# Two of the four weight-quadrant sums of a Winograd feed-forward matmul made by accumulating DMAs instead of VectorE

## Chip, cores, metric

The kernel runs on one core of a Trainium2 chip, as one program. The metric is the device time of one execution in microseconds (us); lower is better. The engines are TensorE (PE: matmuls; PEld: its weight loads), VectorE (DVE), ScalarE (ACT), GpSimd (POOL) and SyncE (SP, which only issues DMAs here).

## What is computed

One layer of a streaming encoder on 512 tokens of width 1024: an adaLN-modulated norm, an input projection that feeds a gMLP branch and an mLSTM branch, an output projection and a gated residual; then the part that matters here, a modulated norm and a squared-ReLU MLP of inner width 4096:

```python
xn = modulate(rmsnorm(h, norm2_g[l]), sh2, sc2)
ff = jnp.square(jax.nn.relu(xn @ w_ff1[l])) @ w_ff2[l]
h = h + g2[:, None, :] * ff
return rmsnorm(h, final_g)
```

`xn` is 512 x 1024, `w_ff1` 1024 x 4096, `w_ff2` 4096 x 1024, all in 32-bit floats.

## The kernel before

Every large matmul runs in three passes. Each operand is split into a high part, rounded to PE's fp32r format by a cast on ScalarE, and a low part, the difference, from VectorE; `mm3` (lines 106 to 109) then issues high x high, high x low and low x high into one PSUM bank. A weight piece of 512 KB is thus loaded by SP into a staging buffer (pool `raws`, tag "raw", three buffers), cast (line 908 in the changed part: wh), subtracted (line 909: wl) and used. The pairs wh and wl have three buffers each.

The first feed-forward matmul, `xn @ w_ff1`, is done in eight groups n of 512 of the 4096 columns. Group 0 is multiplied directly (`block0`, banks f10b, weight splits f100 to f106, activations x2h/x2l), first for the first half of the tokens and then for the second. Groups 1 to 7, called blocks below, use Winograd's form of Strassen's algorithm: the weights of a block are cut in quadrants B11, B12, B21, B22 (rows kh by columns nh, each held as 128 partitions x 4 x 256), the activations in A11 (first tokens, first half of the width), A12, A21 (second tokens), A22, and seven products replace eight:

- activation sums, made once ahead of the loop: S1 = A21 + A22, S2 = S1 - A11, S3 = A11 - A21, S4 = A12 - S2 (line 974, split in lines 976 and 977);
- weight sums, made per block by VectorE: T1 = B12 - B11 (line 928), T2 = B22 - T1 (line 930), T3 = B22 - B12 (line 934), T4 = B21 - T2 (line 937);
- products in this order, each 24 matmuls of 128x256 in one PSUM bank (`product`): P1 = A11 B11, P6 = S2 T2, P2 = A12 B21, P7 = S3 T3, P5 = S1 T1, P4 = A22 T4, P3 = S4 B22;
- the results are put together from the banks by one copy on ScalarE (line 1005) and six additions on VectorE (lines 1006 to 1016), and `relu2` applies relu and square on ScalarE.

`operands()` is a generator that yields the split operands in the order of the products; `product` draws them so that the split of an operand is ordered three products ahead of its use, and its cast waits until the product three places ahead of it has released its wh buffer. The loads of a block's quadrants are issued two at a time at two places of the block before (`load_quads`, line 902). B11 and B21 go to the staging buffers (tag "raw", 3), B12 and B22 to pool `x2p` (tag "q", 3). T1 and T2 take the two buffers of tag "sc" in pool `fp`, which held the scaled token tiles `sc2` of the norm (`resid_norm`, lines 814 to 825: the residual is added in lines 819 and 820, squared and summed in 822, GpSimd makes the reciprocal root in lines 72 and 73, and VectorE scales in line 824). T3 is written over B12.

A scheduler orders the instructions of each engine when the program is built. On the chip every engine runs its list in order, and so do the two that issue DMAs: an instruction that waits holds up all that stands behind it on that engine. Names with numbers, such as T21, are a tile and its block: T2 of block 1.

Of the kernel before, what the change touches and what calls it, by code (L numbers as in the profile page):

```python
# [16 lines left out]
P = 128  # L17
# [29 lines left out]
def block_kernel(ctx, tc, vecs_d, rows_d, ws_d, x_d, w_ada, w_in, w_out, w_ff1, w_ff2, out_d):  # L47
    nc = tc.nc
    act, dve, pool, pe, sp = nc.scalar, nc.vector, nc.gpsimd, nc.tensor, nc.sync

    const = ctx.enter_context(tc.tile_pool(name="const", bufs=1))
    raws = ctx.enter_context(tc.tile_pool(name="raws", bufs=3))
# [665 lines left out]
    for half in range(2):  # L718
# [4 lines left out]
        if half == 0:  # L723
            for t in range(TB):
                dve.scalar_tensor_tensor(out=vg[t], in0=vg[t], scalar=gmv[:, t, 0:1], in1=lng,
                                         op0=ALU.subtract, op1=ALU.mult)
                dve.scalar_tensor_tensor(out=vg[t], in0=vg[t], scalar=grs[:, t:t + 1], in1=lnb,
                                         op0=ALU.mult, op1=ALU.add)
        for t in range(TB):
            act.activation(ug[t][:, cs], b[t], AF.Gelu_apprx_tanh)  # L730
        for g in range(4 * half, 4 * half + 4):
# [33 lines left out]
    fp = ff.enter_context(tc.tile_pool(name="ffp", bufs=1))  # L765
# [36 lines left out]
    for k in range(KT):  # L802
# [35 lines left out]
    x2p = x2s.enter_context(tc.tile_pool(name="x2p", bufs=1, side="right"))  # L838
# [9 lines left out]
    def ring(nm, dt=F32, shape=(2, 256)):  # L848
        return fp.tile([P] + list(shape), dt, tag="hT", name=nm, bufs=32)
# [19 lines left out]
    def half_op(pr, kh):  # L869
        return lambda kt: tuple(v[:, kt % 2] for v in x2[pr, 2 * kh + kt // 2])  # L870
# [7 lines left out]
    for k0 in range(0, KT, 2):  # L878
        raw = raws.tile([P, 2, 512], F32, tag="raw", name=f"raw_f10{k0}")
# [15 lines left out]

    hq = {}

    def quad(n, kh, nh):
        pl_, tg, bf = (x2p, "q", 3) if nh else (raws, "raw", 3)
        raw = pl_.tile([P, 4, 256], F32, tag=tg, name=f"B{n}{kh}{nh}", bufs=bf)  # L900
        c0 = n * 512 + nh * 256
        sp.dma_start(out=raw, in_=w_ff1[kh * 512:(kh + 1) * 512, c0:c0 + 256].rearrange("(k p) c -> p k c", p=P))
        return raw

    def op_split(src, nm):
        wh = wpool.tile([P, 4, 256], F32R, tag="wh", name="wh_" + nm)
        wl = wpool.tile([P, 4, 256], F32R, tag="wl", name="wl_" + nm)
        act.copy(out=wh, in_=src)  # L908
        dve.tensor_sub(out=wl, in0=src, in1=wh.bitcast(F32))  # L909
        return wh, wl  # L910

    NB = FF // 512
    quads = {}

    def load_quads(n, kh):
        if n < NB:
            for nh in range(2):
                quads[n, kh, nh] = quad(n, kh, nh)

    def operands():  # L920
        for n in range(1, NB):
            if n == 1:
                load_quads(n, 0)
                load_quads(n, 1)
            b11, b12, b21, b22 = (quads[n, kh, nh] for kh in range(2) for nh in range(2))
            yield op_split(b11, f"B11{n}")
            t1 = fp.tile([P, 4, 256], F32, tag="sc", name=f"T1{n}", bufs=2)
            dve.tensor_sub(out=t1, in0=b12, in1=b11)
            t2 = fp.tile([P, 4, 256], F32, tag="sc", name=f"T2{n}", bufs=2)
            dve.tensor_sub(out=t2, in0=b22, in1=t1)  # L930
            load_quads(n + 1, 0)
            yield op_split(t2, f"T2{n}")
            yield op_split(b21, f"B21{n}")
            dve.tensor_sub(out=b12, in0=b22, in1=b12)
            yield op_split(b12, f"T3{n}")
            yield op_split(t1, f"T1{n}")
            dve.tensor_sub(out=t2, in0=b21, in1=t2)
            yield op_split(t2, f"T4{n}")
            load_quads(n + 1, 1)
            yield op_split(b22, f"B22{n}")  # L940

    ops_ = operands()
    opq = []

# [14 lines left out]
    for k in range(KT):  # L959
        block0(1, k)  # L960

    def relu2(dst, src):
        act.activation(dst, src, AF.Relu)
        act.activation(dst, dst, AF.Square)

    for pr in range(2):
# [2 lines left out]
    sx = {}  # L969
    for kp in range(2):  # L970
        a11, a12, a21, a22 = xn[0, kp], xn[0, kp + 2], xn[1, kp], xn[1, kp + 2]
        for nm, op, dst, i0, i1 in (("S1", dve.tensor_add, a22, a21, a22), ("S3", dve.tensor_sub, a21, a11, a21),
                                    ("S2", dve.tensor_sub, a11, a22, a11), ("S4", dve.tensor_sub, a12, a12, a11)):
            op(out=dst, in0=i0, in1=i1)
            hl = mp.tile([P, 2, 2, 256], F32R, tag="mv", name=f"{nm}hl{kp}", bufs=8)
            act.copy(out=hl[:, 0], in_=dst)
            dve.tensor_sub(out=hl[:, 1], in0=dst, in1=hl[:, 0].bitcast(F32))
            sx[nm, kp] = hl
    prefetch_op(2)
    for pr in range(2):  # L980
        for nh in range(2):
            relu2(hq[0, nh, pr], fb[pr][nh].rearrange("p (f t) -> p f t", f=2))

    def sum_op(nm):
        return lambda kt: tuple(sx[nm, kt // 2][:, q, kt % 2] for q in range(2))

    def product(xop, nm):
        prefetch_op(3)
        wh, wl = opq.pop(0)
        bk = bank(nm)  # L990
        for kt in range(4):
            xh_, xl_ = xop(kt)
            for f in range(2):
                fs = slice(f * P, (f + 1) * P)
                mm3(bk[:, f * 256:(f + 1) * 256], wh[:, kt, fs], wl[:, kt, fs], xh_, xl_, kt == 0 and f == 0,
                    kt == 3 and f == 1)
        prefetch_op(2)
        return bk.rearrange("p (f t) -> p f t", f=2)

    for n in range(1, NB):  # L1000
        c = {(nh, th): ring(f"h{n}{nh}{th}") for nh in range(2) for th in range(2)}
        for key, v in c.items():
            hq[(n,) + key] = v
        c11, c12, c21, c22 = c[0, 0], c[1, 0], c[0, 1], c[1, 1]
        act.copy(out=c11, in_=product(half_op(0, 0), f"P1{n}"))
        dve.tensor_add(out=c12, in0=c11, in1=product(sum_op("S2"), f"P6{n}"))
        dve.tensor_add(out=c11, in0=c11, in1=product(half_op(0, 1), f"P2{n}"))
        relu2(c11, c11)
        dve.tensor_add(out=c21, in0=c12, in1=product(sum_op("S3"), f"P7{n}"))
        p5 = product(sum_op("S1"), f"P5{n}")  # L1010
        dve.tensor_add(out=c22, in0=c21, in1=p5)
        dve.tensor_add(out=c12, in0=c12, in1=p5)
        relu2(c22, c22)
        dve.tensor_add(out=c21, in0=c21, in1=product(half_op(1, 1), f"P4{n}"))
        relu2(c21, c21)
        dve.tensor_add(out=c12, in0=c12, in1=product(sum_op("S4"), f"P3{n}"))
        relu2(c12, c12)

    ws_ff = Stream([(w_ff2[k * P:(k + 1) * P, :], 1, D, f"f2{k}") for k in range(FF // P - LAST)], 2)
    ws_ff.prefetch(2)  # L1020
# [52 lines left out]
    for t in range(TB):  # L1073
        sc = fp.tile([P, D], F32, tag="sc", name=f"sc3{t}", bufs=2)
        zs = []
        for hf in range(2):
# [70 lines left out]
```

## Time and profile before

| what | value |
|---|---|
| median of 2 runs | 835.91 us (835.77 to 836.05) |
| span of the profiled execution, first to last instruction | 834.4 us |
| PE busy, share of the span | 822.7 us, 99% |
| VectorE busy | 553.4 us, 66% |
| ScalarE busy | 359.5 us, 43% |
| GpSimd busy | 42.2 us, 5% |
| mean granted TensorE clock | 0.995 |
| 512 KB quadrant loads of the changed loop | 28, median 3.8 us to landing |

The runs list no separate time of the profiled execution; its span stands 1.5 us below the median of the runs. Times in the text are us from the start of that span. In the profile, a group's row gives busy time and mean ns, then the engine's idle time ahead of the group and what ended it; a timeline row gives the start, the duration, the engine, the line, the operation and what it writes and reads; tile names there carry no numbers. The loop over blocks 1 to 7 runs from 506.7 to about 648 us, some 20.2 us a block.

### The profile page before, as it was taken

What the parts mean: (1) busy time and instruction counts of PE and PEld (TensorE: products, weight loads), DVE (VectorE), ACT (ScalarE), POOL (GpSimd) and SP (SyncE); (2) the same over time, 40 slices, a digit from 0 to 9 for tenths busy, and PEclk for the clock granted to TensorE, in tenths of its full rate; (3) what the DMA queues carried; (4) which work ended last, traced back from release to release, by engine and by line L of the source; (5) the groups of instructions that cost most, each with busy time, mean ns of one, the idle gap of its engine ahead of it and who ended that gap; (6) DMA issues with size and microseconds to landing.
All of it is one profiled execution on the core that took longest, in us unless ns stands there. A gap on an engine that the chain in (4) does not pass through costs nothing.

```text
span 834.4 us, 11373 instructions
## 1 busy us (share of the span) xinstructions
PE 822.7 (99%) x4427; PEld 700.2 (84%) x4427; DVE 553.4 (66%) x857; ACT 359.5 (43%) x540; POOL 42.2 (5%) x60
## 2 busy tenths in 40 slices
PE   8999999999999999999999999999999999999996
PEld 6887888887888888888888899999999888888885
DVE  5979657584733377888566689888888434443546
ACT  5557456274333233222444456666666221221314
POOL 2003020130100000100000000000000000000000
PEclk9999999999999999999999999999999999999998
DMA  9973331143033398676344231333321422222302
GB/s 274 269 239 107 105 97 26 43 135 101 3 98 101 114 340 290 211 266 218 106 179 144 84 122 49 105 108 114 106 77 65 138 101 101 78 99 101 111 15 102
DMA packets 66822, 107.28 MB, mean 129 GB/s; under 512 B 5328, under 2 KB 38224, under 8 KB 66768
## 3 DMA queue, kind: packets, MB, share of 16 engines
q1 hardware_dynamic: 66768, 106.56, 39.6%
q8 instruction: 35, 0.57, 0.3%
q14 instruction: 19, 0.16, 0.1%
HBM read 104.44 MB, written 2.10 MB: 128 GB/s over the span
## 4 chain that ended last, share of the span: by engine, by line
PE 94%; ACT 1%; DMA 1%; issue 1%; DVE 1%; POOL 0%; SPq 0%; POOLq 0%; DVEq 0%
PE ob L108 7%; PE ob L109 7%; PE ob L107 7%; PE P L107 6%; PE P L108 6%; PE P L109 6%; PE qk L273 4%; PE wo L107 1%; PE wo L108 1%; PE wo L109 1%; PE cp L232 1%; PE k1b L107 1%; PE u1b L107 1%; PE mv1b L109 1%; PE gb0b L108 1%
## 5 line engine op out<-in xcount | busy, mean ns | idle before, releaser
L107 PE MATMUL ob<-wh_f,hsh 128*128 128x512 f32 x240 | 94.9, 395 | 0.0
L108 PE MATMUL ob<-wl_f,hsh 128*128 128x512 f32 x240 | 94.9, 395 | 0.0
L109 PE MATMUL ob<-wh_f,hsl 128*128 128x512 f32 x240 | 94.9, 395 | 0.0
L85 ACT CAST wh_f<-raw_f 128x1024 fp32r<-128x1024 f32 x28 | 29.5, 1053 | 115.2 <-PE ob L109 112.1
L86 DVE TENSOR_TENSOR wl_f<-raw_f,wh_f 128x1024 fp32r<-128x1024 f32 x28 | 34.3, 1225 | 58.2 <-ACT wh_f L85 57.1
L107 PEld LDWEIGHTS ob<-wh_f,hsh 128*128 128x128 f32 x240 | 45.2, 188 | 10.8
L108 PEld LDWEIGHTS ob<-wl_f,hsh 128*128 128x128 f32 x240 | 45.2, 188 | 10.8
L109 PEld LDWEIGHTS ob<-wh_f,hsl 128*128 128x128 f32 x240 | 45.2, 188 | 10.8
L908 ACT CAST wh_T<-T 128x1024 fp32r<-128x1024 f32 x21 | 22.0, 1049 | 24.3 <-PE P L108 23.4
L107 PE MATMUL P<-x2h,wh_B 128*128 128x256 f32 x112 | 31.7, 283 | 0.0
L108 PE MATMUL P<-x2l,wh_B 128*128 128x256 f32 x112 | 31.6, 282 | 0.0
L109 PE MATMUL P<-x2h,wl_B 128*128 128x256 f32 x112 | 31.4, 280 | 0.0
L908 ACT CAST wh_B<-B 128x1024 fp32r<-128x1024 f32 x21 | 22.1, 1051 | 18.1 <-PE P L108 16.7
L1027 DVE CAST hsh<-h 128x512 fp32r<-128x512 f32 x30 | 12.7, 426 | 25.6 <-PE ob L108 25.6
L909 DVE TENSOR_TENSOR wl_T<-T,wh_T 128x1024 fp32r<-128x1024 f32 x21 | 25.7, 1225 | 2.9 <-ACT wh_T L908 2.9
L909 DVE TENSOR_TENSOR wl_B<-B,wh_B 128x1024 fp32r<-128x1024 f32 x21 | 25.6, 1221 | 0.5 <-ACT wh_B L908 0.5
L86 DVE TENSOR_TENSOR wl_gb<-raw_gb,wh_gb 128x1024 fp32r<-128x1024 f32 x8 | 9.8, 1224 | 20.7 <-ACT wh_gb L85 20.7
L1028 DVE TENSOR_TENSOR hsl<-h,hsh 128x512 fp32r<-128x512 f32 x30 | 20.7, 691 | 3.0 <-DVE hsh L1027 0.5
L651 DVE SCALAR_TENSOR_TENSOR accg<-arg,c_act,accg 128x1024 f32<-128x1024 f32 x14 | 17.9, 1282 | 5.2 <-DMA arg<-in_w_ada 5.0
L109 PEld LDWEIGHTS P<-x2h,wl_B 128*128 128x128 f32 x112 | 21.3, 190 | 0.0
L108 PEld LDWEIGHTS P<-x2l,wh_B 128*128 128x128 f32 x112 | 21.0, 188 | 0.0
L107 PEld LDWEIGHTS P<-x2h,wh_B 128*128 128x128 f32 x112 | 20.9, 187 | 0.0
(544 smaller groups left out, 2492.3 us busy)
## 6 DMA issues: line engine op xcount, KB each, us to landing
raw_f<-in_w_ff SPq DMA_DIRECT2D x36, 512.0 KB, 3.3
B<-in_w_ff SPq DMA_DIRECT2D x28, 512.0 KB, 3.8
ar<-in_w_ada SPq DMA_DIRECT2D x64, 128.0 KB, 3.4
arg<-in_w_ada SPq DMA_DIRECT2D x16, 512.0 KB, 5.6
raw_o<-in_w_in SPq DMA_DIRECT2D x8, 512.0 KB, 3.7
raw_mv<-in_w_in SPq DMA_DIRECT2D x8, 512.0 KB, 3.5
raw_gb<-in_w_in SPq DMA_DIRECT2D x8, 512.0 KB, 3.6
raw_v<-in_w_in SPq DMA_DIRECT2D x8, 512.0 KB, 3.5
```

The lines of the kernel that those rows point to most:

```text
L85: act.copy(out=wh, in_=raw)
L86: dve.tensor_sub(out=wl, in0=raw, in1=wh.bitcast(F32))
L107: pe.matmul(out, lhsT=ah, rhs=bh, start=start, stop=False)
L108: pe.matmul(out, lhsT=ah, rhs=bl, start=False, stop=False)
L109: pe.matmul(out, lhsT=al, rhs=bh, start=False, stop=stop)
L232: pe.matmul(cps[c][:, o:o + 1], lhsT=tile_[:, vi, f * P:(f + 1) * P], rhs=rhs, start=first and q == 0, stop=last and q == len(todo) - 1)
L273: pe.matmul(bk, lhsT=wx[:, kk, f * P:(f + 1) * P], rhs=xx[k], start=k == 0 and ps_ == 0, stop=k == KT - 1 and ps_ == 2)
L651: dve.scalar_tensor_tensor(out=acc, in0=raw, scalar=c_act[:, k:k + 1], in1=acc, op0=ALU.mult, op1=ALU.add)
L908: act.copy(out=wh, in_=src)
L909: dve.tensor_sub(out=wl, in0=src, in1=wh.bitcast(F32))
L1027: dve.tensor_copy(out=h_, in_=src)
L1028: dve.tensor_sub(out=l_, in0=src, in1=h_.bitcast(F32))
```

## The change

VectorE no longer makes T1 and T3. Signs are turned so that both are plain sums, T1 = B11 + B12 and T3 = B12 + B22. For each of them SP loads the first quadrant into the tile, and then a DMA issued by GpSimd loads the second with `accum_op=ALU.add`, which adds to what lies there. T2 = B22 + T1 and T4 = B21 + T2 stay on VectorE as additions. B11, B21 and B22 are still loaded by themselves, B12 is not; a block now takes seven loads of 512 KB instead of four. The activation sums become S1 = A22 - A21, S3 = A11 - A21, S2 = -A11 - S1 and S4 = -A12 - S2; two of the four result quadrants come out negated, which the relu takes up with a scale of -1.

```diff
+    def quad(pl_, tg, bf, nm, *parts):
+        raw = pl_.tile([P, 4, 256], F32, tag=tg, name=nm, bufs=bf)
+        sp.dma_start(out=raw, in_=quad_of(*parts[0]))
+        for part in parts[1:]:
+            pool.dma_start(out=raw, in_=quad_of(*part), accum_op=ALU.add)
         return raw
...
-    def load_quads(n, kh):
+    def load_early(n):
         if n < NB:
-            for nh in range(2):
-                quads[n, kh, nh] = quad(n, kh, nh)
+            quads[n, "T1"] = quad(fp, "sc", 2, f"T1{n}", (n, 0, 0), (n, 0, 1))
+            quads[n, "B11"] = quad(raws, "raw", 3, f"B11{n}", (n, 0, 0))
+
+    def load_late(n):
+        if n < NB:
+            quads[n, "B22"] = quad(x2p, "q", 3, f"B22{n}", (n, 1, 1))
+            quads[n, "B21"] = quad(raws, "raw", 3, f"B21{n}", (n, 1, 0))
+            quads[n, "T3"] = quad(x2p, "q", 3, f"T3{n}", (n, 0, 1), (n, 1, 1))
...
             yield op_split(b11, f"B11{n}")
-            t1 = fp.tile([P, 4, 256], F32, tag="sc", name=f"T1{n}", bufs=2)
-            dve.tensor_sub(out=t1, in0=b12, in1=b11)
             t2 = fp.tile([P, 4, 256], F32, tag="sc", name=f"T2{n}", bufs=2)
-            dve.tensor_sub(out=t2, in0=b22, in1=t1)
-            load_quads(n + 1, 0)
+            dve.tensor_add(out=t2, in0=b22, in1=t1)
             yield op_split(t2, f"T2{n}")
             yield op_split(b21, f"B21{n}")
-            dve.tensor_sub(out=b12, in0=b22, in1=b12)
-            yield op_split(b12, f"T3{n}")
+            yield op_split(t3, f"T3{n}")
             yield op_split(t1, f"T1{n}")
-            dve.tensor_sub(out=t2, in0=b21, in1=t2)
+            dve.tensor_add(out=t2, in0=b21, in1=t2)
+            load_early(n + 1)
             yield op_split(t2, f"T4{n}")
-            load_quads(n + 1, 1)
+            load_late(n + 1)
             yield op_split(b22, f"B22{n}")
...
-        relu2(c22, c22)
+        relu2(c22, c22, -1.0)
...
-        relu2(c12, c12)
+        relu2(c12, c12, -1.0)
```

In the new order T1 and T2 of a block take the two "sc" buffers as before, and T3 goes round in the three "q" buffers with B22; the load of T1 of block n + 1 takes the buffer of T1 of block n.

The instructions move at three places that the prediction speaks of. The first is GpSimd's list just ahead of the loop, where rs2 is the reciprocal root of one token tile's norm, made tile after tile:

```order
 L72 TENSOR_SCALAR rs2_3767<-ss2_3766 128x1
 L73 TENSOR_TENSOR rs2_3767<-rs2_3767,mhalf_79 128x1
+L906 DMA T31_4563<-in_w_ff1 128x4x256
 L72 TENSOR_SCALAR rs2_3767<-ss2_3766 128x1
 L73 TENSOR_TENSOR rs2_3767<-rs2_3767,mhalf_79 128x1
 L72 TENSOR_SCALAR rs2_3767<-ss2_3766 128x1
 L73 TENSOR_TENSOR rs2_3767<-rs2_3767,mhalf_79 128x1
```

The pairs shown are those of token tiles 1, 2 and 3; the accumulate of T3 of block 1 now stands between tiles 1 and 2. Before, GpSimd had nothing there.

The second is VectorE's list at the same time, where x2h1k and x2l1k are the split activations of the second tokens and sc23 is the scaled token tile 3. Before:

```order
L820 TENSOR_TENSOR yb_86<-yb_86,rt13_4266 128x512
L928 TENSOR_TENSOR T11_4566<-B101_4556,B100_4554 128x1024
L934 TENSOR_TENSOR B101_4556<-B111_4560,B101_4556 128x1024
L824 TENSOR_SCALAR sc23_4269<-yb_86,rs2_3767 128x1024
L930 TENSOR_TENSOR T21_4568<-B111_4560,T11_4566 128x1024
L865 CAST x2h10_4397<-xn10_4394 128x512
L866 TENSOR_TENSOR x2l10_4398<-xn10_4394,x2h10_4397 128x512
L909 TENSOR_TENSOR wl_T21_4575<-T21_4568,wh_T21_4574 128x1024
L865 CAST x2h11_4404<-xn11_4401 128x512
```

And now:

```order
L820 TENSOR_TENSOR yb_86<-yb_86,rt13_4266 128x512
L824 TENSOR_SCALAR sc23_4269<-yb_86,rs2_3767 128x1024
L865 CAST x2h10_4397<-xn10_4394 128x512
L866 TENSOR_TENSOR x2l10_4398<-xn10_4394,x2h10_4397 128x512
L938 TENSOR_TENSOR T21_4570<-B221_4559,T11_4554 128x1024
L865 CAST x2h11_4404<-xn11_4401 128x512
L866 TENSOR_TENSOR x2l11_4405<-xn11_4401,x2h11_4404 128x512
L913 TENSOR_TENSOR wl_T21_4573<-T21_4570,wh_T21_4572 128x1024
L865 CAST x2h12_4411<-xn12_4408 128x512
```

The two subtractions are gone, and the sum T2 has moved behind the first pair of activations, ahead of the second.

The third is SP's list, from the first load of T1 of block 1 to that of block 3, now:

```order
L904 DMA T11_4554<-in_w_ff1 128x4x256
L904 DMA B113_4922<-in_w_ff1 128x4x256
L904 DMA T32_4720<-in_w_ff1 128x4x256
L904 DMA T12_4681<-in_w_ff1 128x4x256
L904 DMA B223_4954<-in_w_ff1 128x4x256
L904 DMA B213_4956<-in_w_ff1 128x4x256
L904 DMA B114_5160<-in_w_ff1 128x4x256
L904 DMA T33_4958<-in_w_ff1 128x4x256
L904 DMA T13_4919<-in_w_ff1 128x4x256
```

Five loads a block stand here, each behind the release of its buffer; T11 stands behind the loads of B11 and B21 of blocks 1 and 2. The two accumulates of each block follow one another on GpSimd's list, T3 ahead of T1.

More of the change, by code (lines that the diff above doesn't have):

```diff
@@ L896, in block_kernel, with quad_of @@
     hq = {}
-    def quad(n, kh, nh):
-        pl_, tg, bf = (x2p, "q", 3) if nh else (raws, "raw", 3)
-        raw = pl_.tile([P, 4, 256], F32, tag=tg, name=f"B{n}{kh}{nh}", bufs=bf)
+    def quad_of(n, kh, nh):
         c0 = n * 512 + nh * 256
-        sp.dma_start(out=raw, in_=w_ff1[kh * 512:(kh + 1) * 512, c0:c0 + 256].rearrange("(k p) c -> p k c", p=P))
+        return w_ff1[kh * 512:(kh + 1) * 512, c0:c0 + 256].rearrange("(k p) c -> p k c", p=P)
+    def quad(pl_, tg, bf, nm, *parts):
[3 more added lines that the diff above has]
+            pool.dma_start(out=raw, in_=quad_of(*part), accum_op=ALU.add)
         return raw
@@ L922, in operands @@
             if n == 1:
-                load_quads(n, 0)
-                load_quads(n, 1)
-            b11, b12, b21, b22 = (quads[n, kh, nh] for kh in range(2) for nh in range(2))
+                load_early(n)
+                load_late(n)
+            t1, b11, b22, b21, t3 = (quads[n, q] for q in ("T1", "B11", "B22", "B21", "T3"))
             yield op_split(b11, f"B11{n}")
-            t1 = fp.tile([P, 4, 256], F32, tag="sc", name=f"T1{n}", bufs=2)
-            dve.tensor_sub(out=t1, in0=b12, in1=b11)
             t2 = fp.tile([P, 4, 256], F32, tag="sc", name=f"T2{n}", bufs=2)
-            dve.tensor_sub(out=t2, in0=b22, in1=t1)
-            load_quads(n + 1, 0)
+            dve.tensor_add(out=t2, in0=b22, in1=t1)
             yield op_split(t2, f"T2{n}")
             yield op_split(b21, f"B21{n}")
-            dve.tensor_sub(out=b12, in0=b22, in1=b12)
-            yield op_split(b12, f"T3{n}")
+            yield op_split(t3, f"T3{n}")
             yield op_split(t1, f"T1{n}")
-            dve.tensor_sub(out=t2, in0=b21, in1=t2)
+            dve.tensor_add(out=t2, in0=b21, in1=t2)
+            load_early(n + 1)
             yield op_split(t2, f"T4{n}")
-            load_quads(n + 1, 1)
+            load_late(n + 1)
             yield op_split(b22, f"B22{n}")
@@ L960, in block_kernel, with relu2 @@
         block0(1, k)
-    def relu2(dst, src):
-        act.activation(dst, src, AF.Relu)
+    def relu2(dst, src, sign=1.0):
+        act.activation(dst, src, AF.Relu, scale=sign)
         act.activation(dst, dst, AF.Square)
@@ L971, in block_kernel @@
         a11, a12, a21, a22 = xn[0, kp], xn[0, kp + 2], xn[1, kp], xn[1, kp + 2]
-        for nm, op, dst, i0, i1 in (("S1", dve.tensor_add, a22, a21, a22), ("S3", dve.tensor_sub, a21, a11, a21),
-                                    ("S2", dve.tensor_sub, a11, a22, a11), ("S4", dve.tensor_sub, a12, a12, a11)):
-            op(out=dst, in0=i0, in1=i1)
+        for nm, dst in (("S1", a22), ("S3", a21), ("S2", a11), ("S4", a12)):
+            if nm == "S1":
+                dve.tensor_sub(out=dst, in0=a22, in1=a21)
+            elif nm == "S3":
+                dve.tensor_sub(out=dst, in0=a11, in1=a21)
+            elif nm == "S2":
+                dve.scalar_tensor_tensor(out=dst, in0=a11, scalar=-1.0, in1=a22, op0=ALU.mult, op1=ALU.subtract)
+            else:
+                dve.scalar_tensor_tensor(out=dst, in0=a12, scalar=-1.0, in1=a11, op0=ALU.mult, op1=ALU.subtract)
             hl = mp.tile([P, 2, 2, 256], F32R, tag="mv", name=f"{nm}hl{kp}", bufs=8)
```

## The prediction

> **What bounds the kernel now.** I read the page first, then busy time by stretch, the waits of TensorE, the chain that ended last, and the timelines of single engines around the first feed-forward matmul.
>
> ```profile
> span 834.4 us, 11373 instructions
> PE 822.7 (99%) x4427; PEld 700.2 (84%) x4427; DVE 553.4 (66%) x857; ACT 359.5 (43%) x540; POOL 42.2 (5%) x60
> ```
>
> TensorE has work nearly all the time. Inside the changed loop one block n is seven products of 24 matmuls. The stretch below is one whole block (n = 2), with the busy time of PE, PEld, DVE, ACT and POOL after its length:
>
> ```profile
> core 0: us, PE busy (x) PEld busy (x) DVE busy (x) ACT busy (x) POOL busy (x), PEclk, DMA share, GB/s
> 526.85:547.01 20.16, 20.16 (x171) 20.16 (x170) 17.31 (x19) 12.79 (x16) 0.00 (x0) 1.00 0.35 105
> ```
>
> PE and its weight loads fill 20.16 of 20.16 us at full clock, one product in 2.88 us. VectorE is busy 17.31 us, much, but it isn't what PE waits for. The list of waits of the weight loads holds a single wait on another engine between 440 and 660 us:
>
> ```profile
> PEld tr L846 <- DVE sc L824: 0.3, 1, 0.3
> ```
>
> So in the loop nothing but fewer matmuls could make the kernel faster, and the change removes none. It can only lose, wherever an operand comes later than PE wants it. The one wait above lies just ahead of the loop, where the chain of the end leaves PE and runs through other engines without slack:
>
> ```profile
> 477.98 1.30 DVE f102l L782 x2
> 479.30 5.09 DMA B<-in_w_ff
> 484.41 1.07 ACT wh_B L908
> 485.65 1.00 issue
> 486.65 0.70 DVE yb L820
> 487.37 1.16 ACT sc L822 x2
> 488.60 1.21 POOL rs L72
> 489.89 0.58 POOL rs L73
> 490.49 0.76 DVE sc L824
> 491.30 1.09 PE tr L846 x8
> ```
>
> This reads: a staging buffer comes free after f102l, B11 of block 1 is loaded and split, VectorE then adds the residual of the last token tile, its norm goes through ScalarE and GpSimd, and PE transposes. Whatever makes f102l late makes PE late by as much.
>
> **Part 1: sums taken off VectorE, signs.** Lines 928 and 934 go:
>
> ```profile
> L928 DVE TENSOR_TENSOR T<-B,B 128x1024 f32<-128x1024 f32 x7 | 8.6, 1226 | 0.2
> L934 DVE TENSOR_TENSOR B<-B,B 128x1024 f32<-128x1024 f32 x7 | 8.5, 1220 | 0.0
> ```
>
> That is 8.6 + 8.5 = 17.1 us of VectorE, all of it under PE's full stretch: worth 0, at most PE's few gaps (last rival). The sign flips turn four additions of 128x512 into another form and put a scale on activations that run anyway: 0.
>
> **Part 2: the price of an accumulating load.** The trace has no DMA issued by GpSimd, so I bound two numbers: G, how long GpSimd is held by one issue, and X, from the start of that issue to the landing of 512 KB. Rows: plain 512 KB loads in the loop, three such loads issued in one go at 466.13, the slowest 512 KB load of the page, a GpSimd instruction over 512 elements per partition.
>
> ```profile
> DMA to landing us min/median/max: 3.6/3.6/3.8
> ```
> ```profile
> L902 SPq DMA_DIRECT2D B<-in_w_ff x3: 368/500/500, 466.1 to 467.1; - x3
> ...
> DMA to landing us min/median/max: 3.9/5.0/5.9
> ```
> ```profile
> rowg<-in_rows SPq DMA_DIRECT2D x2, 512.0 KB, 6.2
> ```
> ```profile
> L426 POOL TENSOR_TENSOR k4l<-cvk,k4h 128x512 fp32r<-128x512 f32 x1 | 1.8, 1817 | 1.6 <-ACT k4h L425 1.6
> ```
>
> G lies between SP's 0.4 us (the 368 ns above) and all of X, if GpSimd were held until the landing. The load has 512 pieces of 1 KB, so I take the 1.8 us of the GpSimd row, the only one that shows software at work on such a count. X cannot be under a plain load, 3.6; above I put two passes at the slowest row, 2 x 6.2 = 12.4. I take 3.6 - 0.4 + 1.8, and for reading the old contents one more pass at the rate of loads that follow each other: issues half a microsecond apart land 1.5 apart (466.13 + 3.9 = 470.0, about 466.55 + 5.0 = 471.55, 467.1 + 5.9 = 473.0). X = 6.5 us (an estimate from these rows).
>
> **Part 3: GpSimd's first accumulate stands ahead of a norm.** In the new order GpSimd issues the accumulate of T3, block 1, before the rsqrt of token tile 2. It waits for T3's first load, which takes the place of the second of the three loads at 466 and lands at 471.55. GpSimd is then held till 471.55 + 1.8 = 473.35. Before, the rsqrt began at 472.14 and VectorE waited for it:
>
> ```profile
> 472.14 0.22 POOL L72 TENSOR_SCALAR rs<-ss 128x1 f32<-128x1 f32 x1 [9.47 <-ACT sc L822]
> ```
> ```profile
> 473.05 0.76 DVE L824 TENSOR_SCALAR sc<-yb,rs 128x1024 f32<-128x1024 f32 x1 [0.84 <-POOL rs L73]
> ```
>
> So it comes d = 473.35 - 472.14 = 1.2 us late. Behind it on VectorE stand the splits of xn and of f100 to f104, back to back up to f102l, and behind f102l the chain quoted above: PE loses 1.2 us (none with G = 0.4; G - 0.6 in general). The Trainium skill speaks against the placing too: "SBUF — State Buffer", section "Who interferes with whom", says that copy, cast and tensor_scalar on VectorE can lock GpSimd out of the shared SBUF ports, which starves its descriptors. By it the 0.76 us scaling could hold G up and the sum would be 0.8 us more; in the loop VectorE's rows here are two-input operations, which it exempts, and no run here shows it yet.
>
> **Part 4: T1 of block 1.** Its first load stands on SP behind B21 of block 2, which needs the buffer that wl_B11 frees:
>
> ```profile
> 485.50 1.23 DVE L909 TENSOR_TENSOR wl_B<-B,wh_B 128x1024 fp32r<-128x1024 f32 x1 [0.49 <-ACT wh_B L908]
> ```
> ```profile
> L902 SPq DMA_DIRECT2D B<-in_w_ff x4: 368/368/368, 479.3 to 488.5; - x4
> ...
> DMA to landing us min/median/max: 3.6/4.4/5.2
> ```
>
> Issue at 485.50 + 1.23 + 0.4 = 487.15 + d, landing 4.4 later at 491.55 + d. GpSimd is done with the last norm at 489.89 + 0.58 + d, so it starts at once: T1 is there at L = 498.05 + d. On VectorE the sum T2 = B22 + T1 now stands between the splits of x2h10/x2l10 and x2h11/x2l11, and in order: if T1 is late, x2l11 is late, and PE needs it for the second matmul of k = 2:
>
> ```profile
> 497.38 0.69 DVE L866 TENSOR_TENSOR x2l<-xn,x2h 128x512 fp32r<-128x512 f32 x1
> ```
> ```profile
> 498.13 0.38 PE L108 MATMUL f10b<-x2l,f102h 128*128 128x256 f32 x1
> ```
>
> Before, x2l was ready at 498.07 and PE took it at 498.13: no slack. Now it is ready after the sum, the cast and the subtraction, 1.2 + 0.4 + 0.7 = 2.3 us behind L: 500.35 + d, a stall of 2.3. Two pairs on, x2l12 waits for T2's cast on ScalarE, two activations and T4's sum, L + 5.7 = 503.75 + d, where PE would be at 503.15 + d: 0.6 more. Together X - 3.6 = 2.9 us; 0 at X = 3.6, 8.8 at 12.4.
>
> **Part 5: the loop.** T1 of block n + 1 takes the buffer that wl_T1 of block n frees. PE's product 3 of block 2 starts at 532.57, T1 is split then, and T2 of block 3 has to be split for the product that starts at 549.85:
>
> ```profile
> 532.57 0.28 PE L107 MATMUL P<-x2h,wh_B 128*128 128x256 f32 x1
> ```
> ```profile
> 533.73 1.23 DVE L909 TENSOR_TENSOR wl_T<-T,wh_T 128x1024 fp32r<-128x1024 f32 x1 [0.20 <-ACT wh_T L908]
> ...
> 545.25 1.23 DVE L909 TENSOR_TENSOR wl_T<-T,wh_T 128x1024 fp32r<-128x1024 f32 x1 [0.28 <-ACT wh_T L908]
> ```
> ```profile
> 550.09 0.28 PE L109 MATMUL P<-S2hl,wl_T 128*128 128x256 f32 x1
> ```
> ```profile
> L908 ACT CAST wh_T<-T 128x1024 fp32r<-128x1024 f32 x21 | 22.0, 1049 | 24.3 <-PE P L108 23.4
> ```
>
> Buffer free at 534.96, load issued 535.0, landed 538.6. GpSimd's other accumulate (T3) started one product earlier, at 535.7, and held it till 537.5, so this one starts at once and lands at 538.6 + 6.5 = 545.1. The sum 1.23 (as L928), the cast 1.05 (row below) and the subtraction 1.23 with hops make 3.6, and wl_T must be whole at 550.09: T1 is due at 546.5. Spare 1.4 us. T3's accumulate, T1's first load and the loads that follow share the DMA engines; I take half of the 1.5 us by which loads in one go delay each other: spare 0.65, and the break-even is X = 7.15. At X = 6.5 the loop costs 0, its cover PE's five products in between. Beyond 7.15 each of six blocks (2 to 7) pays the excess, since the next buffer comes free later by the same stall. Under the late sum VectorE also queues the evacuations of products; PE has eight banks, so they cost nothing of their own. The 21 more loads of 512 KB raise the DMA share from 0.35 to about 7/4 of it, 0.6: no bound.
>
> **Sum**, against the profiled span: 834.4 + 1.2 + 2.9 + 0 = 838.5. The median of the runs shown, 835.91, lies 1.5 above the span: 840.0 us.
>
> **Rivals.**
>
> The accumulate paces the loop (0.32). If the old contents are read behind the new ones rather than beside them, X is about two landings and an issue, 3.6 + 3.6 + 1.8 = 9 or more, up to 12.4. At X = 10: 1.2 + 6.4 + 6 x 2.85 = 24.7, 860.6 us. It decides from X = 7.15 on, and is over 2% (16.7 us, about what a measurement tells from no change) where 1.2 + X - 3.6 + 6 (X - 7.15) passes 16.7, at X = 8.9. For it: two passes through the same 16 engines, which a plain load keeps at a share of 0.35 already. Against: the first pass takes only 1.5 us per 512 KB when loads overlap.
>
> A cheap accumulate (0.15): G near 0.4, X near a plain load, 4.1: d = 0, 0.5 in the first block, 836.4 us. For it: GpSimd is idle in the loop (0.00 above), and DMA engines are free two thirds of the time. Against: the pieces are generated by software and every byte of the target is read as well. The Trainium skill is on this side: "DMA: Bandwidth & Descriptors", section "Anatomy of one DMA — SWDGE (gpsimd) path", fits 2.0 us plus bytes over 436 GB/s, with the bytes counted twice an estimate of 4.4 us, by which parts 3 to 5 would give 2.0 and the time 837.9.
>
> VectorE's relief is worth something after all (0.03): the gaps at 491.3 and 498.1, some 0.4 us, close: 835.5 us. Against it: T2's new place in the queue sits in that very gap. That the accumulates are not made at all is excluded: the new order of GpSimd has 14 of them.
>
> **How the numbers follow.** My forecast, the first block pays and the loop hides the rest, has 0.50 with 840.0 us, own range 837 to 845. A quarter of the 0.32 of the pacing rival stays under 2% (X up to 8.9), so slower by over 2% gets 0.24. Within 2%: 0.50 + 0.08 + 0.15 + 0.02 = 0.75; faster 0.01 for what I don't see. The range: below, the cheap case with next to nothing, 836.0; above, X = 10.2, 862.0, which leaves a tenth to each side.
>
> **What would show it.** GpSimd's row for the accumulate (G) and its landing (X). First block right: the rsqrt of tile 2 starts after T3's issue, near 473.4; PE waits at x2l11 for a sum that waits for T1. Loop right: blocks still 20.16 us long, PE without waits, VectorE some 2.4 us per block less busy. Wrong: blocks of 21 us or more with PE waiting for wl_T2 (pacing rival), or product 1 of block 1 starting no later than the 506.66 us of before (cheap rival).

## The result and the profile after

The changed kernel takes 871.60 us (median of 2 runs, 869.61 and 873.59) against 835.91 us: a ratio of 1.042, 95% interval 1.036 to 1.048. That is slower, by 35.7 us, and lies outside the range of the prediction (836 to 862). The head of the page after:

```profile
span 867.8 us, 11443 instructions
PE 838.9 (97%) x4427; PEld 714.5 (82%) x4427; DVE 538.5 (62%) x843; ACT 356.0 (41%) x540; POOL 59.4 (7%) x74
```

VectorE is busy 14.9 us less (the two sums that went were 17.1), and the span is 33.4 us longer. TensorE has the same 4427 matmuls, but is "busy" 16.2 us more: the same work ran slower, and it also stood still. Four lines of the list of waits between 470 and 680 us (total, times, longest) say where it stood:

```profile
DVE T L938 <- DMA T<-in_w_ff: 37.3, 7, 8.2
PE P L107 <- ACT wh_T L912: 10.9, 4, 4.5
PE f10b L107 <- DVE x2h L865: 4.1, 1, 4.1
PE P L109 <- DVE wl_T L913: 2.5, 4, 0.8
```

Line 107 and line 109 wait for the two halves of a split T (in the loop this is T2, the operand of a block's second product), and the sum behind that split (line 938, T2 = B22 + T1) waits in all seven blocks for the accumulating load of T1. The first block has one stall of 4.1 us, and four of the six other blocks have one each, in two parts: 1.94 + 0.76, 1.74 + 0.76, 2.79 + 0.53 and 4.47 + 0.47, together 13.5 us.

The chain of waits ahead of the first of these four, block 2 (start, length, what; PE's pieces left out here):

```profile
526.43 1.18 POOL T L906
527.61 0.49 issue
528.10 9.83 DMA T<-in_w_ff
537.93 0.02 issue
537.95 1.24 DVE T L938
...
539.27 1.05 ACT wh_T L912
540.32 0.02 issue
540.35 1.24 DVE wl_T L913
```

GpSimd issues T3's accumulate at 526.43, T1's at 528.10, and T1 lands 9.83 us later; sum, cast and subtraction follow at once, and PE stands for them. All 14 accumulates by their line (nanoseconds that GpSimd is held, then microseconds from issue to landing, min/median/max):

```profile
L906 POOL DMA_DIRECT2D T<-in_w_ff x14: 1273/1282/1487, 473.2 to 653.7; - x14
...
DMA to landing us min/median/max: 6.0/6.6/11.0
```

G is 1.28 us (I took 1.8). Of the eight accumulates that do not follow close behind another (seven of T3, and T1 of block 1), seven landed after 5.96 to 6.74 us (I took 6.5 for X) and one, T3's in block 6, after 8.05. But T1 landed after 9.83, 10.3, 10.0 and 10.96 us in blocks 2, 3, 4 and 6, where its issue came 1.25 to 2.03 us behind T3's. In blocks 5 and 7 it came 2.6 and 3.0 us behind, landed after 6.98 and 6.36, and those blocks have no stall. (The distance alone does not decide it; see the last section.)

The second half of the loss is in the granted clock (busy time by stretch; the figure after the five engines is the clock):

```profile
core 0: us, PE busy (x) PEld busy (x) DVE busy (x) ACT busy (x) POOL busy (x), PEclk, DMA share, GB/s
499.81:503.22 3.41, 0.00 (x0) 0.00 (x0) 1.51 (x2) 0.25 (x1) 0.00 (x0) 1.00 0.36 56
503.22:510.05 6.83, 6.58 (x29) 6.28 (x30) 6.75 (x12) 6.63 (x12) 0.00 (x0) 0.50 0.00 1
537.36:540.77 3.41, 1.47 (x11) 1.15 (x10) 2.25 (x3) 1.50 (x2) 0.00 (x0) 1.00 0.20 71
540.77:547.60 6.83, 6.07 (x29) 5.98 (x29) 5.59 (x7) 5.27 (x8) 0.00 (x0) 0.50 0.27 78
547.60:551.00 3.40, 3.40 (x30) 3.40 (x30) 1.90 (x2) 1.06 (x2) 0.00 (x0) 1.00 0.70 199
```

Behind the stall of the first block and behind each of the four in the loop the clock is 0.50 for 3.41 or 6.83 us: 29 matmuls in 6.83 us where 30 took 3.40 us right after. There are five such stretches, 4 x 6.83 + 3.41 = 30.7 us, half of which is lost. The account: 4.06 (first block) + 13.5 (loop) + 15.4 (clock) = 32.9 of 33.4 us. It is a rough one. Three of the short second stalls lie inside stretches at half clock, so some 0.9 us are counted twice, and 1.0 us of the 33.4 was lost in the first 110 us of the span, where nothing was changed. Taken from PE's first matmul of one part to that of the next, group 0, in whose last part the first block's stall lies, is 7.5 us longer than before (32.5 against 25.0) and the loop 24.8 (166.0 against 141.3).

### The profile page after: what moved, and what is told of

It is laid out like the page before. It is cut to its first block, busy times and chain, and to the rows that moved or that the text cites. A ratio compares the mean times of both kernels' runs of the same rounds, so it can differ in the third digit from the quotient of the medians.

```text
span 867.8 us, 11443 instructions
## 1 busy us (share of the span) xinstructions
PE 838.9 (97%) x4427; PEld 714.5 (82%) x4427; DVE 538.5 (62%) x843; ACT 356.0 (41%) x540; POOL 59.4 (7%) x74
## 4 chain that ended last, share of the span: by engine, by line
PE 83%; DMA 9%; DVE 3%; ACT 2%; issue 1%; POOL 1%; POOLq 0%; ACTq 0%; DVEq 0%
DMA T<-in_w_ff 8%; PE ob L109 7%; PE ob L107 7%; PE ob L108 7%; PE qk L273 4%; PE P L109 3%; PE P L107 2%; PE P L108 2%; PE wo L107 2%; PE wo L108 2%; PE wo L109 2%; ACT wh_T L912 1%; DVE wl_T L913 1%; PE k1b L107 1%; PE cp L232 1%
## 5 line engine op out<-in xcount | busy, mean ns | idle before, releaser
L912 ACT CAST wh_T<-T 128x1024 fp32r<-128x1024 f32 x28 | 29.3, 1045 | 68.0 <-DVE T L938 48.5
L913 DVE TENSOR_TENSOR wl_T<-T,wh_T 128x1024 fp32r<-128x1024 f32 x28 | 34.3, 1225 | 6.8 <-ACT wh_T L912 6.5
L938 DVE TENSOR_TENSOR T<-B,T 128x1024 f32<-128x1024 f32 x7 | 8.6, 1225 | 37.3 <-DMA T<-in_w_ff 37.3
L107 PE MATMUL P<-S2hl,wh_T 128*128 128x256 f32 x56 | 20.1, 358 | 10.9 <-ACT wh_T L912 10.9
L906 POOL DMA_DIRECT2D T<-in_w_ff x14 | 18.2, 1303 | 156.1 <-DMA T<-in_w_ff 46.3
L107 PEld LDWEIGHTS P<-S2hl,wh_T 128*128 128x128 f32 x56 | 14.4, 257 | 11.8 <-ACT wh_T L912 11.8
L109 PE MATMUL P<-S2hl,wl_T 128*128 128x256 f32 x56 | 20.2, 362 | 2.5 <-DVE wl_T L913 2.5
```

What stands on the lines that cost most here:

```text
L107: pe.matmul(out, lhsT=ah, rhs=bh, start=start, stop=False)
L109: pe.matmul(out, lhsT=al, rhs=bh, start=False, stop=stop)
L906: pool.dma_start(out=raw, in_=quad_of(*part), accum_op=ALU.add)
L938: dve.tensor_add(out=t2, in0=b22, in1=t1)
```

## Experiments

Theory A: T1 comes too late for its place (its buffer comes free late, its accumulate stands behind T3's), and each stall halves TensorE's clock. Rivals: B, any accumulate is too long for T1's place; C, the 21 added loads cost as such; and for the clock, that the accumulates' traffic lowers it and not the stalls. A ratio is against the kernel before in the same set of runs (median 837.33 us in the first four, 838.08 in the others).

**T3 alone.** T1 is a VectorE sum again, T3 accumulates into the B12 tile behind it.

```diff
-            quads[n, "T1"] = quad(fp, "sc", 2, f"T1{n}", (n, 0, 0), (n, 0, 1))
...
-            quads[n, "T3"] = quad(x2p, "q", 3, f"T3{n}", (n, 0, 1), (n, 1, 1))
+            quads[n, "T3"] = quad(x2p, "q", 3, f"T3{n}", (n, 0, 1))
...
+            t1 = fp.tile([P, 4, 256], F32, tag="sc", name=f"T1{n}", bufs=2)
+            dve.tensor_add(out=t1, in0=t3, in1=b11)
+            pool.dma_start(out=t3, in_=quad_of(n, 1, 1), accum_op=ALU.add)
```

> Only T3 is summed by an accumulating DMA (B22 is added to the B12 tile after VectorE has read it for T1 = B11 + B12); 7 accumulates. Theory A (the loss is T1's lateness, T3's sum has two products of slack): PE has no gap over 0.5 us in the loop, no half-clock stretch; GpSimd's first accumulate now stands inside the norm of token tile 3, which can cost up to 2 us once: span 834.4 to 837, median 836 to 838.5. Theory C (traffic or GpSimd's descriptors as such slow the other loads enough): the six blocks of 20.16 us become 21 us or more, median 841 and above.

Measured: 838.07 us, ratio 1.0014 (1.0002 to 1.0027). Busy time over 124 us of the loop:

```profile
526.00:650.00 124.00, 124.00 (x1035) 124.00 (x1035) 100.44 (x109) 78.58 (x101) 6.41 (x5) 1.00 0.48 119
```

PE is busy 124.00 of 124.00 us at full clock beside seven accumulates, as A has it; C is out for this half. The one cost is where my part 3 looked for it. GpSimd now issues T3's first accumulate between the two operations of a norm:

```profile
491.59 0.22 POOL L72 TENSOR_SCALAR rs<-ss 128x1 f32<-128x1 f32 x1 [15.22 <-ACT sc L822]
492.43 1.48 POOL L938 DMA_DIRECT2D T<-in_w_ff  x1 [0.62 <-issue]
493.46 1.07 POOL L73 TENSOR_TENSOR rs<-rs,mhalf 128x1 f32<-128x1 f32 x1
```

PE waits 0.80 us for the transpose behind it.

**T1 alone.** T3 is a VectorE sum over the plain B12 load.

```diff
-            quads[n, "T3"] = quad(x2p, "q", 3, f"T3{n}", (n, 0, 1), (n, 1, 1))
+            quads[n, "T3"] = quad(x2p, "q", 3, f"T3{n}", (n, 0, 1))
...
+            dve.tensor_add(out=t3, in0=t3, in1=b22)
```

> Only T1 is summed by an accumulating DMA; T3 = B12 + B22 is made by VectorE again, in the B12 tile, so GpSimd issues 7 accumulates, never two close together. Theory A (T1's accumulate is slow because it is issued 1.3 to 2.0 us behind T3's and shares the DMA engines with it: 9.8 to 11.0 us there, 6.4 to 7.0 us in the two blocks where they were further apart): T1's issue-to-landing time is 6.0 to 7.0 us in all blocks, PE has no gap over 0.5 us inside the loop and no half-clock stretch there; what stays is the first block (a gap of 4.1 us and 3.4 us of half-clock loss): span about 834.4 + 1 + 4 + 3.4 = 843, median 844. Theory B (an accumulate by itself is too slow for T1's due time): the gaps stay in most blocks, span 860 or more. Theory C (every one of the 21 added loads costs something as such): a third of them is gone, so about a third of the 33 us comes back, span near 857.

Measured: 851.51 us, ratio 1.0173 (1.0156 to 1.0189), span 849.6. X is as A has it, 6.4 to 6.9 us in all blocks, and there is no half clock in the loop. The first block keeps a stall of 4.89 us and a half-clock stretch of 6.83. But the loop is still 5.8 us longer than before (147.1 against 141.3), and A had said a span of 843: PE's weight loads wait ten times for a split, 0.2 to 1.1 us each, 5.3 in all. Half of that is T1: its chain in one block reads

```profile
544.59 4.59 DMA T<-in_w_ff
...
549.25 0.49 issue
549.74 6.54 DMA T<-in_w_ff
```

that is 4.59 + 0.56 + 6.54 = 11.7 us from the first load's issue to the landing, against the 11.5 us (535.0 to 546.5) that the prediction had worked out as T1's due time, and the weight loads then wait 0.2 to 1.0 us for the split of T2 in five blocks, 2.8 us in all. So even a lone accumulate just misses: B holds to that size. The other half belongs to this experiment: T3's sum waits on VectorE for the plain B12 load, with the split of T4 behind it in the queue.

**The same issues, without adding.** The second load overwrites the first, so this kernel leaves out both sums.

```diff
-            pool.dma_start(out=raw, in_=quad_of(*part), accum_op=ALU.add)
+            pool.dma_start(out=raw, in_=quad_of(*part))
```

> The same 14 loads are issued by GpSimd at the same places, but they overwrite their target and do not add, so the sums T1 and T3 are left out (T1 holds B12 alone, T3 holds B22 alone). Theory A with the accumulate's own length as the cause of the long landing (it takes 102 ns for each 1 KB packet where a plain load takes 46): landing 3.7 to 5.5 us after the issue, two of them behind each other under 7 us, no PE gap over 0.5 us in the loop, and in the first block a gap of 4.1 - 2.2 = 1.9 us with 0 to 3.4 us of half clock: span 836 to 840. Rival (the place of the issues, the dispatch and the two loads one behind the other cost it, whatever they do with the old contents): landings stay at 8 us or more where two meet, gaps in most blocks, span above 855.

Measured: 848.98 us (843.94 to 852.91), ratio 1.014 (1.010 to 1.019); the profiled execution is the quickest, span 842.2. The other three took 5 to 9 us more at a lower mean clock (0.987 to 0.992 against 0.995), and no trace shows where. Its line:

```profile
L906 POOL DMA_DIRECT2D T<-in_w_ff x14: 748/750/980, 472.8 to 629.5; - x14
...
DMA to landing us min/median/max: 4.1/4.6/6.1
```

So the adding itself is worth 0.5 us of GpSimd and about 2 us of X alone, and 4 to 5 us of T1's X where two follow each other (5.2 to 6.1 here, 9.8 to 11.0 there). No half clock in this execution's loop, and three stalls of 0.4 to 0.7 us; the first block keeps a stall of 2.35 us and 3.41 us at half clock. A's size was too good (836 to 840 expected): with loads that only overwrite, T1's chain is still 4.82 + 0.57 + 5.76 = 11.2 us in block 3, at the edge.

**T1's product ahead of T3's.** T1's buffer then comes free one product earlier, and GpSimd issues T1's accumulate first.

```diff
-            yield op_split(t3, f"T3{n}")
             yield op_split(t1, f"T1{n}")
+            yield op_split(t3, f"T3{n}")
...
-        dve.tensor_add(out=c21, in0=c12, in1=product(sum_op("S3"), f"P7{n}"))
-        p5 = product(sum_op("S1"), f"P5{n}")
-        dve.tensor_add(out=c22, in0=c21, in1=p5)
-        dve.tensor_add(out=c12, in0=c12, in1=p5)
+        dve.tensor_add(out=c22, in0=c12, in1=product(sum_op("S1"), f"P5{n}"))
+        p7 = product(sum_op("S3"), f"P7{n}")
+        dve.tensor_add(out=c21, in0=c12, in1=p7)
+        dve.tensor_add(out=c12, in0=c22, in1=p7)
+        c12, c22 = c22, c12
+        hq[n, 1, 0], hq[n, 1, 1] = c12, c22
```

> All 14 accumulates stay; the products with T1 and with T3 change places (T1 is split fourth and T3 fifth, the two output buffers change roles, the number of VectorE operations is the same), so T1's buffer comes free one product (2.88 us) earlier and its accumulate goes ahead of T3's on GpSimd. Theory A (T1's lateness and its place behind T3's accumulate): T1 lands 2.9 us plus up to 3 us earlier against its due time, no PE gap over 0.5 us in the loop, no half-clock stretch there, T3's accumulate takes 9 to 11 us instead, inside its slack; the first block's gap and its clock loss stay: span about 843, median 844. Theory B' (14 accumulates are more than the DMA engines carry beside the plain loads): the gaps move to T3 or to the B tiles, span 855 or more. Theory C (added loads cost as such): no change, about 868.

Measured: 866.11 us, ratio 1.035 (1.032 to 1.039). A's forecast of 843 fell. T1's X was 6.2 to 6.8 in all but one block (7.4), but the waits name another operand:

```profile
PE P L109 <- DVE wl_B L913: 14.0, 6, 3.5
DVE T L938 <- DMA T<-in_w_ff: 39.4, 7, 8.3
```

and VectorE's timeline in the first of these places shows why:

```profile
529.00 0.69 DVE L1022 TENSOR_TENSOR h<-h,P 128x512 f32<-128x512 f32 x1 [0.69 <-PE P L109]
535.36 1.23 DVE L938 TENSOR_TENSOR T<-B,T 128x1024 f32<-128x1024 f32 x1 [5.67 <-DMA T<-in_w_ff]
536.51 1.22 DVE L913 TENSOR_TENSOR wl_B<-B,wh_B 128x1024 fp32r<-128x1024 f32 x1
...
538.24 1.22 DVE L913 TENSOR_TENSOR wl_B<-B,wh_B 128x1024 fp32r<-128x1024 f32 x1
```

The order of VectorE's instructions is fixed when the kernel is built, and with T1 earlier T2's sum had been put ahead of the splits of B22 and of the next B11. VectorE takes its queue in order, so it stood 5.67 us at the sum, and PE stood for splits whose data had long been there.

**The same, with T2's sum held in its old place.**

```diff
-            dve.tensor_add(out=t2, in0=b22, in1=t1)
+            with tc.issue_after(last[-1].ins):
+                dve.tensor_add(out=t2, in0=b22, in1=t1)
```

(Shown against the run before. `last` collects the subtractions of the splits, and `last[-1]` is the one that made wl_B11; `issue_after` puts the sum behind it in VectorE's order.)

> As the run in which T1's and T3's products change places, but the sum T2 = B22 + T1 is held behind the split of B11 on VectorE, the place that it has in the changed kernel. In the run before, T2's sum had moved ahead of two splits of B tiles on VectorE, which stood there 5.7 us with PE waiting for wl_B behind it. Theory A (T1 comes too late for its place): T1's chain of load, dispatch and accumulate needs 4.8 + 0.6 + 6.4 = 11.8 us and now has 11.3 + 2.9 = 14.2, so no PE gap over 0.5 us in the loop, blocks of 20.2 us, no half-clock stretch there; the first block keeps its gap of 4 to 6 us and 3.4 us of clock loss: span 843 to 845, median 844 to 847. Theory C (the 21 added loads slow everything): gaps stay, blocks of 21 us or more, span above 850.

Measured: 845.82 us, ratio 1.0084 (1.0058 to 1.0110), span 845.3. Two stretches, the first block and the loop:

```profile
499.00:512.00 13.00, 8.75 (x49) 8.25 (x48) 7.72 (x12) 6.35 (x11) 0.00 (x0) 0.74 0.28 41
...
526.00:650.00 124.00, 124.00 (x1036) 124.00 (x1035) 95.52 (x102) 76.69 (x99) 15.35 (x12) 1.00 0.75 173
```

The loop is whole again, 141.3 us long as before, with all 14 accumulates and the same loads, at a DMA share of 0.75. T3's accumulate, now second, takes 9.7 to 10.6 us in five of six blocks, inside its slack. This settles A against C: the loop's loss was T1's time of arrival, and in the run before it the place of T2's sum in VectorE's order (holding it moved other lines of VectorE and ScalarE a little as well). Whether T1 gains more from its buffer coming free earlier or from standing ahead of T3 was not taken apart. What is left is the first block, a stall of 4.11 us and a half-clock stretch of 6.83 us.

**And the first block's T1 and T3 by VectorE** (12 accumulates remain; the change of the two loads is left out here).

```diff
...
+            if n == 1:
+                t1 = fp.tile([P, 4, 256], F32, tag="sc", name=f"T1{n}", bufs=2)
+                dve.tensor_add(out=t1, in0=t3, in1=b11)
+                dve.tensor_add(out=t3, in0=t3, in1=b22)
+            else:
+                t1 = quads[n, "T1"]
```

> As the run before it, and in the first block T1 and T3 are summed by VectorE; 12 accumulates remain, in blocks 2 to 7. If T1's lateness in its two forms (first block; loop) is the whole loss: no PE gap over 0.5 us after 460 us, no half-clock stretch between 20 us and the end, span 834 to 836, ratio to the kernel before between 0.998 and 1.003. If the added loads or GpSimd's descriptors cost something as such: 840 or more. Faster than the kernel before by more than 0.3%: neither theory, since PE is busy all the time.

Measured: 837.63 us, ratio 0.9992 (0.9979 to 1.0006), span 835.9. From 460 us to the end of the loop:

```profile
460.00:526.00 66.00, 66.00 (x489) 61.56 (x488) 51.15 (x75) 35.03 (x59) 6.86 (x10) 1.00 0.36 103
...
526.00:650.00 124.00, 124.00 (x1032) 123.86 (x1031) 96.02 (x104) 77.63 (x100) 12.82 (x10) 1.00 0.69 164
```

And the same 124 us of the loop in the kernel before:

```profile
526.00:650.00 124.00, 124.00 (x1027) 123.60 (x1026) 105.06 (x113) 79.05 (x100) 0.00 (x0) 1.00 0.32 97
```

PE has no gap and a clock of 1.00. So the whole loss is gone, and so is any gain: VectorE is busy 96.0 instead of 105.1 us, and that buys nothing, since PE was full before. No version here beats the kernel before.

**Stalls without accumulates.** The kernel before, with a GpSimd chain that holds up one operand of the second product.

```diff
+        if n > 1:
+            dly = fp.tile([P, 256], F32, tag="dly", name=f"dly{n}", bufs=1)
+            src = hq[n - 1, 1, 0][:, 0]
+            for w in [256] * (WIDTHS[n - 2] // 256) + [WIDTHS[n - 2] % 256]:
...
+                    pool.tensor_scalar(out=dly[:, :w], in0=src[:, :w], scalar1=0.0, scalar2=None, op0=ALU.mult)
+                    src = dly
+            el = sx["S2", 0][:, 1, 0, 0:1]
+            pool.tensor_tensor(out=el, in0=el.bitcast(F32), in1=dly[:, 0:1], op=ALU.add)
```

> The kernel before, with no accumulates; in blocks 2 to 7 a chain of GpSimd operations of growing length, started by the last sum of the block ahead, adds zero to one element that the second product reads, so PE waits there for a time that grows from block to block, planned 0.3 to 3.5 us. Theory A: a gap halves the granted clock whoever causes it, in steps of 3.4 us, from some length on: long gaps (over 2 us) are each followed by 3.4 or 6.8 us at 0.5, the short ones (under 1 us) by none; the time lost is the gaps plus half of those stretches. Rival: the low clock belongs to the accumulating DMAs; here the clock stays 1.00 and the loss is the gaps alone. By the Trainium skill's page on TensorE's clock gate only gaps over about 3.4 us do it; the changed kernel had it at 1.7 + 0.8 us within a window.

Measured: 863.04 us (one run), span 861.2; stalls of 2.08, 1.96, 1.97, 3.26, 2.54 and 3.27 us, so no short ones. Stretches of 3.41 us on the grid at which the clock changes, for the first two:

```profile
531.45:534.86 3.41, 1.69 (x15) 1.48 (x13) 1.88 (x2) 2.61 (x4) 2.05 (x3) 1.00 0.32 96
534.86:538.28 3.42, 3.05 (x25) 3.05 (x26) 0.27 (x1) 0.12 (x1) 0.32 (x1) 1.00 0.69 208
555.34:558.75 3.41, 1.45 (x12) 1.24 (x11) 1.22 (x1) 1.51 (x2) 2.17 (x3) 1.00 0.57 156
558.75:562.17 3.42, 3.42 (x18) 3.42 (x17) 0.00 (x0) 0.15 (x1) 0.00 (x0) 0.50 0.55 151
```

The clock falls with no accumulate in the kernel, behind four of the six stalls, so the stalls do it; the run above with all 14 accumulates, no stall and full clock in the loop says the same from the other side. What counts is not the length alone: the stall of 1.96 us lies whole in one stretch (PE busy 1.45 of 3.41), and the clock halves in the next, as it does behind those of 1.97, 3.26 and 3.27 us. Those of 2.08 and 2.54 us are cut by a border (1.72 and 0.37; 0.98 and 1.56 idle), and nothing follows. By the Trainium skill ("TensorE: Matmul & The Clock Gate", section "HAM oscillation — how this bites in real kernels") a kernel should have no TensorE gap over about 3.4 us; these rows agree with a window of 3.41 us, but show that 1.96 us of idle time in it is enough.

**Work in place of the stall.** The changed kernel with the first product run twice in blocks 2 to 7.

```diff
-        for kt in range(4):
+        for kt in times * list(range(4)):
...
-        act.copy(out=c11, in_=product(half_op(0, 0), f"P1{n}"))
+        act.copy(out=c11, in_=product(half_op(0, 0), f"P1{n}", 2 if n > 1 else 1))
```

> The changed kernel, but in blocks 2 to 7 the 24 matmuls of the first product are run twice into the same bank (the second pass overwrites the first with the same numbers), which is 2.88 us more work for PE in each of six blocks, 17.3 us in all, at the place where PE stood waiting for T2. Theory A (PE's gaps, and the half clock that follows each of them, are the loss): the work fills the gaps, no half-clock stretch in the loop, only the first block's 4.1 + 3.4 us and 1 us stay: span 834.4 + 17.3 + 8.5 = 860, so 8 us less than the changed kernel in spite of more work. Rival (the low clock is caused by the accumulates' traffic or power, not by the gaps): the four half-clock stretches of the loop stay, span 872 or more. Rival (no clock effect, gaps alone): work replaces gaps in four blocks and adds 2 x 2.88 in the two that had none: 873.

Measured: 874.07 us, ratio 1.043 (1.038 to 1.047), span 873.1: A's 860 fell. T1's chain was longer than the fill allowed for (5.54 + 0.56 + 10.15 = 16.3 us in block 3), and stalls of 8.5 us remained in the loop. The clock's part held: of four half-clock stretches in the loop one stayed, where the stall left PE busy 1.07 us of a window, and a window with 2.00 us of work left the clock alone:

```profile
565.81:569.22 3.41, 2.00 (x14) 1.80 (x15) 2.84 (x4) 3.35 (x6) 0.00 (x0) 1.00 0.00 0
589.70:593.11 3.41, 1.07 (x10) 0.87 (x8) 1.82 (x2) 1.01 (x2) 0.00 (x0) 1.00 0.02 5
593.11:599.94 6.83, 6.27 (x27) 5.98 (x28) 5.63 (x6) 5.31 (x9) 0.00 (x0) 0.50 0.20 52
```

The sum: 17.3 of work, 4.9 ahead of and in the first block, 3.4 of its clock, 8.5 and 3.4 in the loop: 37.5 of 38.7 us. The total, 873, is also what the rival without a clock effect named, so the total decides nothing here; the rows do, and they leave the accumulates' traffic out as the cause of the clock, since all 14 are in this run.

## Why the prediction was wrong, step by step

**What bounds the kernel** was right: PE was full, nothing could be won, and VectorE's 17 us were worth 0. The run with 12 accumulates and no stall shows both.

**Part 2, the price**, was right where the accumulate is alone: X 6.0 to 6.7 us (6.5 forecast) in all but one of the eight, 6.4 to 6.9 in the run with T1 alone, G 1.28 (1.8 forecast). I left out a dispatch: GpSimd starts T1's accumulate 0.55 to 0.57 us after the first load has landed, in all seven blocks (527.54 to 528.10 in block 2).

**Part 3** came as told and was then given back. T3's issue held the norm of token tile 2 up to 474.77, where I had 473.35 (1.0 us of the difference this execution had brought along from its first 110 us):

```profile
473.21 1.49 POOL L906 DMA_DIRECT2D T<-in_w_ff  x1 [9.47 <-DVE x2h L865]
474.77 0.22 POOL L72 TENSOR_SCALAR rs<-ss 128x1 f32<-128x1 f32 x1
...
490.75 0.22 POOL L72 TENSOR_SCALAR rs<-ss 128x1 f32<-128x1 f32 x1 [15.10 <-ACT sc L822]
```

But the rsqrt of the last tile took 0.22 us instead of the 1.21 us quoted of before, and PE waited no longer than before (0.1 us). In the kernel before, one of the two sums that went, with two inputs of 128x1024, ran beside it from 488.50 to 489.73, and the GpSimd operation, begun at 488.60, ended just behind it:

```profile
488.50 1.22 DVE L934 TENSOR_TENSOR B<-B,B 128x1024 f32<-128x1024 f32 x1
```

The Trainium skill ("SBUF — State Buffer", section "Who interferes with whom") says that a VectorE instruction with two SBUF inputs contends with a GpSimd instruction that reads SBUF; these rows agree, with 1.0 us. Whether the scaling could hold an issue up stays open: in no run here did one run beside an issue.

**Part 4**, the first block, had the right mechanism and too small a size: 2.9 us forecast, a stall of 4.06 measured. The first load took 5.32 us (I had 4.4) and the dispatch 0.57. And since part 3 was given back, PE was at its place about 1.1 us earlier and waited that much longer. Behind it came 3.4 us for the clock, of which I had nothing.

**Part 5 is the step that failed**: "I take half of the 1.5 us by which loads in one go delay each other: spare 0.65 ... At X = 6.5 the loop costs 0". The due time was right. What had to fit into 11.5 us was not 3.6 + 6.5 and 0.75 of contention, but 4.15 + 0.56 + 9.83 = 14.5 us in block 2. (The due time fits: what this chain took beyond 11.5 us is within 1 us of the stall in all six blocks. Blocks 5 and 7, at 11.7 and 11.2, have none, and block 6, at 16.2, has the longest.) I had named what shares the DMA engines (T3's accumulate, T1's first load, the loads behind), and then priced it from three plain loads, and called the DMA share no bound by its average over a block. While T1 landed in block 2 that share was not 0.6 but full (a packet counts where it starts, so a short stretch can show more than 1):

```profile
532.60:538.00 5.40, 5.40 (x47) 5.40 (x46) 0.05 (x1) 0.00 (x0) 0.00 (x0) 1.00 1.06 255
```

A 1 KB packet of an accumulate took 102 ns in the median and one of a plain load 46. By these numbers an accumulate fills the 16 engines for 512 x 102 ns / 16 = 3.3 us and a plain load for 1.5 us, an estimate. The runs give the price by parts. T1's accumulate beside the B loads but with no other accumulate: 6.4 to 6.9. Second behind an accumulate by 1.45 us, with no B load near (the run with the products changed and the sum not held): 7.5 and 7.7. Both together: 9.8 to 11.0 in four of six blocks. The rival "the accumulate paces the loop" had the right place and, at X = 10, 860.6 us; it was right about the stalls and had the wrong reason, since X alone is 6.5.

**The missing term** is the clock, 15.4 of 33.4 us. The page of before had given no row for it but those of the first and the last 21 us, but I had a forecast of 2.9 us of stall at full load in hand and did not ask what the granted clock does then. With it the rival at X = 10 would have come to 860.6 + 5 x 3 or so, above the result. And without it the result would have been near 871.6 - 15.4 = 856 us, inside the range: the stalls made the forecast of 840.0 wrong, and the clock took the time out of the range.

## What to carry to other kernels

Where TensorE is full, work taken off VectorE is worth nothing, and the question about a change is only which operand now arrives later and how much slack its place has; price a transfer there by its landing beside the transfers that will run with it, not alone. Add to a forecast stall of about 2 us or more the half clock that can follow it, here 1.7 or 3.4 us each. And when a transfer is made earlier, look where the in-order queues now put the instruction that waits for it: one sum moved ahead of two splits in VectorE's queue cost 21 us (spans of 866.4 against 845.3).

## What the runs showed of the hardware

- **The clock window.** After 520 us, over all runs here, every 3.41 us window at full clock with 1.86 us or more of PE idle time was followed by half clock, and none with 1.72 us or less was. In the first block one window with 1.64 us, in stalls and small gaps, was followed by it as well, so the border is near half of the window, not exactly known. How long the low clock lasts goes with PE's idle time in its first window: with 0.53 us or more it lasted two windows in all nine cases, with 0.52 us or less one window in nine of ten (the tenth, 0.25 us in the first block of the changed kernel, had two).
- **Two accumulates close together** do not run side by side at no cost: the second took 7.5 and 7.7 us 1.45 us behind the first with no plain load beside it, where most single ones took 6.0 to 6.9. The distance alone does not decide: 2.5 and 2.6 us behind, the second took 10.6 and 10.0 us with two plain loads that started 0.3 to 0.9 and 3.5 to 4.1 us after it (the run with T2's sum held), but 2.6 us behind it took 7.0 with plain loads 1.4 and 4.5 us after it (block 5 of the changed kernel). What decides between these was not tested. Two loads by GpSimd that only overwrite took 4.1 to 4.4 and 5.2 to 6.1.
- **GpSimd is held** 1.28 us by the issue of an accumulating load of 512 KB and 0.75 us by a plain one; the first issue of a kernel took 0.2 us longer in every run (1.48 or 1.49, and 0.98 us).
